# Moving the end waits for all DMAs from SyncE, ahead of the closing barrier, to GpSimd, between that barrier and the semaphore clearing

## The chip, the cores and the metric

The program runs on one core of a Trainium2 chip. The metric is the device time of one execution in microseconds. Executions of the same program mostly differ by up to about 1 us. The span of a profile is the time from the program's first instruction to its last. It is about 1.8 us shorter than the device time of the same run.

## The reference

The infinity norm of each row of an 8192 x 8192 float32 matrix, that is the largest absolute value of each row.

```python
def setup_inputs():
    rows = 8192
    cols = 8192
    return {"x": np.random.randn(rows, cols).astype(np.float32)}

def reference(x):
    return np.linalg.norm(x, ord=np.inf, axis=1)
```

So 268 MB are read once, and 32 KB are written.

## The kernel before

SyncE issues all loads, VectorE reduces each tile with a maximum of absolute values, and the last rows come in smaller and smaller pieces, so that little is left to reduce after the last load. Three stores write the result: `r_bulk` (rows of the large tiles) and `r_tail` from ScalarE's queue, and at the very end `r_fin`, one number per partition, 512 bytes, from SyncE's queue.

```python
    for i in range(0, n_tail, B):
        ...
                if last and k == k_last - 1:
                    absmax(r_tail[:, : n_tail - 1], part[:])
                    nc.scalar.dma_start(
                        out=out_t[:, : n_tail - 1], in_=r_tail[:, : n_tail - 1]
                    )
                    absmax(r_fin[:], t[:, at : B * cols + k_last - 1])
        ...
    nc.sync.dma_start(out=out_t[:, n_tail - 1 :], in_=r_fin[:])
    nc.at_finalize(start_first_load_early)
```

The end of the program is not written in the kernel; the framework adds it. In the built program of before it is, engine by engine. (A drain is the profile's DRAIN: VectorE's starts at 624.28 us, during the last reduction, and ends at 625.00 us, just after it. An event wait is an EVENT_SEMAPHORE instruction that waits for semaphores. A wait is met when its semaphore has the value that it waits for. In the list, 99 is VectorE's semaphore, 100 to 107 are those of the DMAs, 102 is the one that the last store raises, 96 and 97 belong to the barrier.)

```
SyncE : event wait (104, 103) ; event wait (105, 102) ; event wait (106, 101) ;
        event wait (107, 100) ; drain (99)              <- one drain with nine waits, split
all   : first barrier   (each engine: drain, raises 96; GpSimd: gather 96, release 97)
GpSimd: drain ; clear the range of semaphores
all   : second barrier
```

The drain with nine waits stands split in the built program: the drain keeps the first of its list (99), and the other eight go in pairs into event waits ahead of it. The nine waits keep the clearing behind the last update of every DMA's semaphore (the last store raises its own 16 times, and the last of these is called its completion below).

## Time and profile before

| | before |
|---|---|
| device time, median of six runs | 629.20 us (629.04 to 629.80) |
| span of the profiled run | 627.3 us |
| HBM read, rate over the span | 268.44 MB, 428 GB/s |
| VectorE busy | 552.7 us, 88% |
| issue of the last store to its landing | 1.4 us |

The page of the profile. Under it are the busy share of the DMA engines in 40 slices (tenths of a slice) and the rate in each.

```profile
span 627.3 us, 196 instructions
...
DVE 552.7 (88%) x58; POOL 0.2 (0%) x4
...
DMA  9999999999999999999999999999999999999996
GB/s 401 468 401 464 405 460 410 455 414 451 418 451 418 451 418 447 422 447 422 447 422 447 422 447 422 447 422 443 426 420 428 425 433 435 426 429 427 427 425 274
...
HBM read 268.44 MB, written 0.03 MB: 428 GB/s over the span
```

The DMA engines are busy in every slice but the last, at 401 to 468 GB/s, so the kernel is taken to be bound by the reads until its last few microseconds. The profile's chain of what ended last puts 64.1% on loads and 23.5% on the reductions into `r_bulk`, which free the buffers that later loads wait for; the change touches neither. The timeline of those (start, duration, engine, line, operation):

```profile
624.26 0.69 DVE L81 TENSOR_REDUCE r_fin<-t 128x1 f32<-128x517 f32 x1
624.98 0.35 SPq L117 DMA_DIRECT2D out_dram<-r_fin  x1
```

The last reduction ends at 624.96 us, SyncE issues the store at 624.98. The span still has 2.36 us to go. The view of waits for SyncE in the window from 624 us on (who waited for whom: us in total, times, longest):

```profile
SPq L117 <- DVE r_fin L81: 12.1, 1, 12.1
SPq L144 <- DMA out_dram<-r_fin: 1.0, 1, 1.0
SPq L144 <- PEq L144: 0.6, 2, 0.4
```

SyncE waits 1.0 us for the store (the second row); the third row is the two barriers. The instructions of the closing line, SyncE's from 625.43 to 626.45 us and then all of GpSimd's after 626 us (count, shortest/median/longest ns, first and last start):

```profile
L144 SPq EVENT_SEMAPHORE  x1: 968/968/968, 625.5 to 625.5; - x1
```

```profile
L144 POOLq EVENT_SEMAPHORE  x4: 17/17/17, 626.7 to 627.2; - x4
L144 POOLq DRAIN  x2: 34/52/70, 626.8 to 627.1; - x2
L144 POOLq EVENT_SEMAPHORE_RANGE_CLEAR  x1: 92/92/92, 626.9 to 626.9; - x1
```

SyncE's event wait of 968 ns holds the store's semaphore. Only after it come GpSimd's gather, which starts at 626.68 us, and its clearing, at 626.94 us.

### The profile page before, as it was taken

Reading aid. Unit: us, or ns where it says so; the run is one execution under the profiler, and the core shown is the slowest. Engines: PE = TensorE matmul, PEld = TensorE weight load, DVE = VectorE, ACT = ScalarE, POOL = GpSimd, SP = SyncE. Lnnn points to the kernel's source line nnn. Section 1 sums busy time; section 2 is a strip of 40 time slices with the busy share of each in tenths; the row PEclk is TensorE's granted clock in tenths of the full one; section 3 lists DMA queues with packets and bytes.
Section 4 is the critical chain, followed back from the end, with each engine's and each line's share of the span. In section 5 each row is a group of like instructions: output and inputs, shape, how many; then the busy total and the mean of one; then the engine's idle time right before and its main releaser. Section 6 shows DMA issues by size and latency. Waiting matters only on the chain.

```text
span 627.3 us, 196 instructions
## 1 busy us (share of the span) xinstructions
DVE 552.7 (88%) x58; POOL 0.2 (0%) x4
## 2 busy tenths in 40 slices
DVE  0588988889988889888898888998889999999998
POOL 0000000000000000000000000000000000000000
DMA  9999999999999999999999999999999999999996
GB/s 401 468 401 464 405 460 410 455 414 451 418 451 418 451 418 447 422 447 422 447 422 447 422 447 422 447 422 443 426 420 428 425 433 435 426 429 427 427 425 274
DMA packets 9138, 268.49 MB, mean 428 GB/s; under 512 B 1968, under 2 KB 1968, under 8 KB 2352
## 3 DMA queue, kind: packets, MB, share of 16 engines
q1 hardware_dynamic: 8208, 268.44, 99.2%
q10 hardware_dynamic: 928, 0.03, 0.1%
q14 instruction: 2, 0.02, 0.0%
HBM read 268.44 MB, written 0.03 MB: 428 GB/s over the span
## 4 chain that ended last, share of the span: by engine, by line
DMA 64%; DVE 30%; another core or an unknown queue 4%; issue 1%; SPq 0%
DMA t<-in_x_dram 64%; DVE r_bulk L81 24%; DVE part L81 5%; DVE t L81 1%; SPq L100 0%; DVE r_fin L81 0%
## 5 line engine op out<-in xcount | busy, mean ns | idle before, releaser
L81 DVE TENSOR_REDUCE r_bulk<-t 128x2 f32<-128x16384 f32 x24 | 413.3, 17220 | 69.7 <-DMA t<-in_x_dram 69.7
L81 DVE TENSOR_REDUCE part<-t 128x1 f32<-128x4096 f32 (+2 forms) x26 | 130.0, 5067 | 1.3 <-DMA t<-in_x_dram 1.3
L81 DVE TENSOR_REDUCE t<-t 128x1 f32<-128x2048 f32 (+2 forms) x5 | 8.6, 1746 | 0.3 <-DMA t<-in_x_dram 0.3
L78 DVE MEMSET part<- 128x60 f32 x1 | 0.1, 108 | 0.9 <-PEq L133 0.9
L81 DVE TENSOR_REDUCE r_fin<-t 128x1 f32<-128x517 f32 x1 | 0.7, 691 | 0.0
L81 DVE TENSOR_REDUCE r_tail<-part 128x15 f32<-128x60 f32 x1 | 0.2, 216 | 0.0
L133 POOL MEMSET const-bfloat16-1.0<- 128x1 bf16 x1 | 0.1, 101 | 0.0
L133 POOL MEMSET const-uint8-127<- 128x1 uint8 x1 | 0.1, 101 | 0.0
L133 POOL MEMSET const-float32-0.0<- 128x1 f32 x1 | 0.1, 98 | 0.2 <-issue 0.2
L133 POOL MEMSET const-float32-1.0<- 128x1 f32 x1 | 0.1, 98 | 0.0
## 6 DMA issues: line engine op xcount, KB each, us to landing
t<-in_x_dram SPq DMA_DIRECT2D x8, 4096.0 KB, 37.0
t<-in_x_dram SPq DMA_DIRECT2D x10, 2048.0 KB, 30.4
t<-in_x_dram SPq DMA_DIRECT2D x11, 1024.0 KB, 24.6
t<-in_x_dram SPq DMA_DIRECT2D x1, 512.0 KB, 15.9
t<-in_x_dram SPq DMA_DIRECT2D x2, 256.0 KB, 13.2
t<-in_x_dram SPq DMA_DIRECT2D x24, 40.7
out_dram<-r_bulk ACTq DMA_DIRECT2D x1, 24.0 KB, 57.9
out_dram<-r_tail ACTq DMA_DIRECT2D x1, 7.5 KB, 5.6
```

Source lines behind the costliest of these rows:

```text
L78: nc.vector.memset(part[:], 0.0)
L81: nc.vector.reduce_max(out=o, in_=i, axis=X, apply_absolute_value=True)
L133: nc = _bacc.Bacc("TRN2", target_bir_lowering=False, num_devices=1)
```

## The change

The intent: run the first barrier while the last store is still under way, and let only the clearing wait for the DMAs, on the reading that only the clearing needs them. The nine waits are taken off SyncE and put on a drain of GpSimd that takes the place of the drain ahead of the clearing. They are sorted so that the store's semaphore (`lane`) is the last of the list. SyncE's drain goes, and the drain ahead of the clearing is replaced, so the program has one drain fewer.

```diff
+def wait_for_stores_on_pool(nc):
+    sp, pool = mybir.EngineType.SP, mybir.EngineType.Pool
+    body, end = nc.main_func.blocks[-2:]
+    last_store = [ ... SyncE's DMA copies ... ][-1]
+    lane = last_store.sync_info.on_update[0].id
+    insts = end.instructions
+    src = next(i for i in insts if i.engine == sp)
+    ...
+    clear = next(k for k, i in enumerate(insts) if type(i).__name__ == "InstISA")
+    dst = insts[clear - 1]
+    ...
+    waits = sorted(src.sync_info.on_wait, key=lambda s: s.id == lane)
+    assert waits[-1].id == lane
+    wait = mybir.InstDrain(
+        name=nc.get_next_instruction_name(),
+        engine=pool,
+        ins=[],
+        outs=[],
+        sync_info=mybir.SyncInfo(on_wait=waits, on_update=[]),
+    )
+    insts = insts[: clear - 1] + [wait] + insts[clear:]
+    end.instructions = [i for i in insts if i.name != src.name]
 ...
     nc.at_finalize(start_first_load_early)
+    nc.at_finalize(wait_for_stores_on_pool)
```

In the built program this gives:

```
SyncE : (nothing)
all   : first barrier
GpSimd: event wait (105, 104) ; event wait (106, 103) ; event wait (107, 101) ;
        event wait (102, 100) ; drain (99) ; clear
all   : second barrier
```

## The prediction

> **What bounds the kernel.** HBM reads. The page shows 268.44 MB at a mean of 428 GB/s over a 627.3 us span, DMA in the 9s in every slice but the last. VectorE is busy 552.7 us (88%) and waits for loads. The change touches only the last 2 us.
>
> **The end now** (instructions of the closing line, by engine, and semaphore events, profiled run). VectorE ends r_fin at 624.97. SyncE issues the 512-byte store at 624.98, to 625.33. Its packets are done at about 626.03, its 16 completions arrive from 626.23 to 626.40. SyncE's drain with nine waits stands as four event waits of two semaphores each and a drain. The store's semaphore is in the second, which sits 968 ns, to 626.42. Then follow two more event waits (626.46, 626.52), the drain (626.59), SyncE's barrier drain (626.65), GpSimd's gather and release (626.68, 626.76), GpSimd's drain (626.84, 70 ns), the clearing (626.94, 92 ns) and the second barrier; the last instruction ends at 627.32. So 0.54 us pass from the store's last completion to the clearing, and 0.38 us from there to the end.
>
> **What the change does.** It removes SyncE's nine waits from ahead of the first barrier and puts them on a GpSimd drain between release and clearing, in place of the drain there, the store's semaphore sorted last. By the split seen before (the drain keeps the list's first wait, VectorE's; the rest go in pairs ahead of it) I expect the store's wait in the fourth of four event waits on GpSimd, directly ahead of the drain. Loads, reductions and stores stay.
>
> - First barrier: SyncE arrives at about 625.4 instead of 626.65; VectorE has arrived at 625.01. GpSimd releases by about 625.55. Three satisfied event waits at GpSimd's spacing of about 80 ns (626.68 to 626.76) end by about 625.85, 0.5 us before the store lands: hidden.
> - New chain after the last completion (626.40): GpSimd wakes and goes on, 0.1 us (before: last gather arrival 626.654 to the next event 626.756); drain to clearing 0.1 us (626.837 to 626.936). Clearing at about 626.60 instead of 626.94.
> - The second barrier is unchanged, 0.38 us.
>
> Saved: 0.54 - 0.20 = 0.34 us, all on the critical path, an estimate from these durations. The store's flight of 1.4 us stays exposed. The Trainium skill ("DMA: Bandwidth & Descriptors", Anatomy of one DMA) puts most of a DMA's fixed cost in the write receipt before the semaphore fires; here 0.2 to 0.37 us pass from the last packet to the completions.
>
> **Time.** 629.22 - 0.34 = 628.9 us, range 628.2 to 629.8. The three runs of before span 0.76 us, twice the gain, so a few runs may not resolve it. Faster by over 2% (12.6 us): 0.005. Within 2%: 0.99. Slower by over 2%: 0.005.
>
> **What would show it.** SyncE's 968 ns event wait is gone; GpSimd has one of 0.5 to 0.6 us in its fourth event wait; from r_fin's end to the last instruction 2.0 us instead of 2.35. Loads and reductions are unchanged.
>
> **What would make it wrong.** GpSimd wakes much slower from a DMA's semaphore than SyncE; the waits are lowered in another order, so that several 80 ns events follow the landing (gain down to 0.1 us); the store completes later; or the drift of reads between runs, up to about 1 us, covers the gain.

## The result, and the profile after

| | before | after |
|---|---|---|
| device time, median (range) of six runs | 629.20 us (629.04 to 629.80) | 628.88 us (628.68 to 629.48) |
| ratio, 95% interval | | 0.9994 (0.9981 to 1.0007) |
| span of the profiled run | 627.3 us | 627.2 us |
| end of the last reduction to the last instruction | 2.362 us | 2.003 us |
| last completion of the store to the clearing | 0.539 us | 0.174 us |

A ratio is the mean time of one kernel's runs over that of the other's of the same rounds, so it is not quite the ratio of the medians.

The page after:

```profile
span 627.2 us, 194 instructions
...
DVE 552.7 (88%) x58; POOL 0.2 (0%) x4
...
DMA  9999999999999999999999999999999999999996
...
HBM read 268.44 MB, written 0.03 MB: 428 GB/s over the span
```

Loads and reductions are as before. The span is only 0.09 us shorter, because in this profile the last reduction ended 0.27 us later, which the timeline shows beside that of before:

```profile
624.53 0.69 DVE L113 TENSOR_REDUCE r_fin<-t 128x1 f32<-128x517 f32 x1
625.25 0.35 SPq L149 DMA_DIRECT2D out_dram<-r_fin  x1
```

So the spans of two single profiles can't be subtracted here; the tail, from the end of this reduction, can. The waits of SyncE in the window from 624 us on:

```profile
SPq L149 <- DVE r_fin L113: 12.1, 1, 12.1
SPq L177 <- PEq L177: 1.3, 2, 1.2
```

SyncE no longer waits for the store. What it has instead is a wait of 1.2 us in a barrier, put down to the engine whose arrival the profile places last. That is the second barrier, which GpSimd now holds up. The instructions of SyncE's closing line from 625.5 to 626.01 us, then GpSimd's event waits (the compiler gives those that it split off a line of its own file), then GpSimd's other closing instructions from 625.9 us on:

```profile
L177 SPq DRAIN  x1: 123/123/123, 625.7 to 625.7; - x1
L177 SPq EVENT_SEMAPHORE  x1: 17/17/17, 625.9 to 625.9; - x1
```

```profile
bacc.py:44 POOLq EVENT_SEMAPHORE  x4: 43/43/43, 626.0 to 626.7; - x4
```

```profile
L177 POOLq EVENT_SEMAPHORE  x3: 17/17/17, 625.9 to 627.1; - x3
L177 POOLq EVENT_SEMAPHORE_RANGE_CLEAR  x1: 92/92/92, 626.8 to 626.8; - x1
L177 POOLq DRAIN  x1: 34/34/34, 627.0 to 627.0; - x1
```

The barrier's release at 625.9 us comes before the store has landed, the four event waits span from 626.0 to 626.7 us, and the clearing follows at 626.8. In full, from the records and the semaphore events of the two traces, counted from the end of the last reduction (us):

```
                                          before    after
store is issued                           +0.027   +0.027
SyncE arrives at the first barrier        +1.697   +0.556
GpSimd releases the first barrier         +1.800   +0.659
GpSimd's third event wait ends                 -   +0.976
store's last completion arrives           +1.441   +1.447
clearing starts                           +1.980   +1.621
last instruction of the program ends      +2.362   +2.003
last update of semaphore 2                +4.265   +3.908
```

The last row is outside the program's span. The Trainium skill ("Runtime: NRT & Kernel Launch", Semaphores 0–2 are reserved) says that semaphore 2 is the runtime's sync barrier, and in the trace its updates are the last events of an execution. From the first instruction to this last update are 629.22 us before, where the run's device time was 629.1 us. The difference is 0.12 us (0.118 to 0.127) in all 13 profiled runs, so this row is a way to see in one trace what the measured time sees. From the last instruction to it are 1.903 us before and 1.905 us after: what the tail lost, the execution, counted from the end of the last reduction, lost too.

### The profile page after: what moved, and what is told of

Read it like the earlier page. It is cut to its first block, busy times and chain, and to the rows that moved or that the text cites. A ratio compares the mean times of both kernels' runs of the same rounds, so it can differ in the third digit from the quotient of the medians.

```text
span 627.2 us, 194 instructions
## 1 busy us (share of the span) xinstructions
DVE 552.7 (88%) x58; POOL 0.2 (0%) x4
## 4 chain that ended last, share of the span: by engine, by line
DMA 64%; DVE 30%; another core or an unknown queue 4%; issue 1%; SPq 0%
DMA t<-in_x_dram 64%; DVE r_bulk L113 24%; DVE part L113 5%; DVE t L113 1%; SPq L132 0%; DVE r_fin L113 0%
```

## The experiments

**The theory.** The gain is made of two things. The barrier now runs under the store's flight of 1.42 us and costs nothing (position); and fewer event waits stand between the store's completion and the clearing (order of the waits). **Rivals:** the order alone is the gain (A); the position or the engine alone, the order being without effect (B); GpSimd is quicker to wake, or one hop between engines less is the gain (C); and the difference in time is drift of the reads.

Each kernel of the experiments gave a correct result. The device time is resolved to about 0.13% (0.8 us) by five rounds. "To clearing" is the time from the store's last completion to the start of the clearing. From the clearing to the last instruction it was 0.38 us wherever the second barrier stands. These values come from one profiled execution of each kernel; where a kernel was profiled twice (the change; e4 and e11), they agree to 2 ns.

| kernel | where the waits stand | event waits, from the store's own to the last | to clearing, us | median time, us | ratio (95%) |
|---|---|---|---|---|---|
| before | SyncE, ahead of barrier | 3, and SyncE's drain | 0.539 | | 1 |
| e2_sync_last | SyncE, ahead, sorted | 1, and SyncE's drain | 0.430 | 629.80 | 0.9999 (0.9987 to 1.0012) |
| e5_pool_ahead | GpSimd, ahead, sorted | 1, and a drain | 0.455 | 629.15 | 1.0000 (0.9987 to 1.0012) |
| e3_pool_unsorted | GpSimd, behind | 3, and a drain | 0.311 | 629.51 | 0.9997 (0.9984 to 1.0010) |
| the change (e1_after) | GpSimd, behind, sorted | 1, and a drain | 0.175 | 629.24 | 0.9992 (0.9978 to 1.0006) |
| e4_pool_on_drain | GpSimd, behind, on the drain | the drain alone | 0.087 | 629.24 | 0.9991 (0.9979 to 1.0004) |
| e6_pool_plus8 | the change, 8 event waits in place of 4 | 1, and a drain | 0.174 | 628.82 | 0.9996 (0.9984 to 1.0009) |
| e7_pool_plus24 | the change, 16 in place of 4 | 1, and a drain | 0.766 | 629.53 | 1.0003 (0.9989 to 1.0016) |
| e9_sync_plus8 | before, 4 more on SyncE | 3, SyncE's drain and 4 more | 0.789 | 629.41 | 1.0006 (0.9993 to 1.0018) |
| e10_sync_plus160 | before, 80 more on SyncE | 3, SyncE's drain and 80 more | 5.380 | 634.42 | 1.0076 (1.0064 to 1.0088) |

The first group (e1 to e4) ran on one chip, beside a kernel before of 629.75 us median; e5 to e9 (without e8) on another (629.21 us); e10, e8 and e11 on a third (629.49 us). The runs of before on the third chip hold one of 631.57 us. It lowers the ratios there: without it the ratio of the plain means is 1.0079 for e10, 0.9992 for e8 and 0.9998 for e11.

**e1_after: the change once more** (no edit).

> The change itself, once more, in five rounds. Theory (barrier hidden under the store's flight, and the store's wait directly ahead of the clearing): from the store's last completion to the start of the clearing 0.17 us (0.54 before), from it to the last instruction 0.56 us (0.92 before), and the time 0.2 to 0.5 us under the kernel before of the same rounds (about 0.9994). Rival (the time's difference is only drift of the reads): the same 0.17 us in the trace, but no difference in time.

Measured: 0.175 us to the clearing, 0.556 us to the last instruction, as in the first profile to 1 ns. The mean time is 0.43 us under before (629.22 against 629.65 us). Both intervals, here and in the first comparison, hold 1, so time alone does not settle it.

**e2_sync_last: the order alone.** The edit against the change:

```diff
-        engine=pool,
+        engine=sp,
...
-    insts = insts[: clear - 1] + [wait] + insts[clear:]
-    end.instructions = [i for i in insts if i.name != src.name]
+    at = next(k for k, i in enumerate(insts) if i.name == src.name)
+    end.instructions = insts[:at] + [wait] + insts[at + 1 :]
```

> The nine waits stay on SyncE ahead of the first barrier; only the order changes, the store's wait in the last event wait. Theory (order and position both count): two event waits of 64 ns no longer follow the completion, so last completion to clearing 0.54 - 0.13 = 0.41 us, time about 0.13 us under before. Rival A (order is all of the gain): 0.17 to 0.20 us, time like the change. Rival B (position or engine is all): 0.54 us.

Measured: 0.430 us. The order is worth 0.109 us in SyncE's place, not all of the gain and not nothing: rivals A and B fall. That it is 0.02 us more than the 0.41 expected is explained under e3. The profile's line of the split event waits of this kernel:

```profile
bacc.py:44 SPq EVENT_SEMAPHORE  x4: 28/28/28, 625.5 to 626.5; - x4
```

**e3_pool_unsorted: the position (with the engine), in the order of before.**

```diff
-    waits = sorted(src.sync_info.on_wait, key=lambda s: s.id == lane)
-    assert waits[-1].id == lane
+    waits = list(src.sync_info.on_wait)
```

> The waits on GpSimd after the first barrier as in the change, but in the order of before, so that the store's wait is in the second of four event waits. Theory: two event waits of about 90 ns now follow the completion: completion to clearing 0.17 + 0.18 = 0.35 us, time about 0.19 us under before. Rival A (order is all): 0.54 us. Rival B (position or engine is all): 0.17 us.

Measured: 0.311 us, between the rivals, but 0.04 us less than expected. The event waits of this kernel, to be read beside that of e2:

```profile
bacc.py:44 POOLq EVENT_SEMAPHORE  x4: 42/43/622, 626.5 to 627.4; - x4
```

Here one event wait took 622 ns, while in e2 and in the change all took 28 or 43 ns although one of them waited as long. The difference goes with the place within the pair, in all kernels here, though no run changed that place alone. In (105, 102) the store's semaphore is the second: 105 is met long before, and the instruction starts, holds through the store's flight and ends 30 ns after the completion. In (102, 100) it is the first: the instruction starts 24 ns after the completion, and takes its 43 ns then, so it ends at 67 ns. The change therefore loses 37 ns again that the old order did not have. Two event waits 87 ns apart, less these 37 ns, are 0.137 us, and that is what the change gains over e3 (0.311 less 0.174). The same holds on SyncE: 22 ns after the completion in before, 45 ns in e2, which is the 0.02 us more found there.

**e4_pool_on_drain: the store's wait on the drain itself.**

```diff
-    waits = sorted(src.sync_info.on_wait, key=lambda s: s.id == lane)
-    assert waits[-1].id == lane
+    waits = sorted(src.sync_info.on_wait, key=lambda s: s.id != lane)
+    assert waits[0].id == lane
```

> As the change, but the store's wait is put first in the list, which leaves it on the drain itself; no event wait follows the completion. Theory: 0.024 us to wake and about 0.10 us from the drain's start to the clearing, so 0.12 us instead of 0.17 us; time 0.05 us under the change, which five rounds will not resolve. Rival (a drain that waits is slower to go on than an event wait): 0.17 us or more.

Measured: 0.087 us, less than the 0.12 us expected. Since the drain keeps the first wait of its list, the store belongs first in the list, not last.

**e5_pool_ahead: the engine alone.** GpSimd waits, ahead of the first barrier's gather.

```diff
-    insts = insts[: clear - 1] + [wait] + insts[clear:]
+    gather = next(
+        k
+        for k, i in enumerate(insts)
+        if i.engine == pool and type(i).__name__ == "InstDrain"
+    )
+    insts = insts[:gather] + [wait] + insts[gather + 1 :]
```

> The waits on GpSimd, sorted as in the change, but ahead of the first barrier's gather: the engine changes, the barrier stays behind the store. Theory (the hidden barrier matters): after the completion come the event wait's end and the drain (0.15 us), the gather (0.08), release (0.08) and the drain ahead of the clearing (0.10): about 0.42 us to the clearing, time about 0.12 us under before. Rival C (GpSimd wakes faster, or one hop between engines less, is the gain): 0.17 to 0.20 us.

Measured: 0.455 us, 0.035 us over the 0.42 us expected and 0.025 us more than with the same waits on SyncE (e2). GpSimd as such is no faster at this; rival C falls. Its store's event wait in the profile:

```profile
bacc.py:44 POOLq EVENT_SEMAPHORE  x1: 43/43/43, 626.4 to 626.4; - x1
```

What is gained between this kernel and the change, 0.281 us, is what no longer stands between the waits and the clearing. The gather starts at 626.561 us, the drain ahead of the clearing at 626.720 and the clearing at 626.820. So 0.159 us of these are the gather and release of the barrier, and 0.100 us are that drain, which this kernel still has and whose place the waiting drain takes in the change. No run hid the barrier and kept both drains, so how much of the 0.100 us comes from the drain saved stays open.

**e6_pool_plus8 and e7_pool_plus24: how much fits under the store's flight.** Both put more waits that are met already on GpSimd, ahead of the store's; the compiler merged them in pairs, and eight of them share an event wait with a DMA's semaphore each (the store's is (102, 99) in both).

```diff
+    dve = next(s for s in waits if s.id == waits[0].id)
+    extra = [
+        mybir.InstEventSemaphore( ..., engine=pool, ...,
+            sync_info=mybir.SyncInfo(on_wait=[dve], on_update=[]))
+        for _ in range(8)     # 24 in e7
+    ]
-    insts = insts[: clear - 1] + [wait] + insts[clear:]
+    insts = insts[: clear - 1] + extra + [wait] + insts[clear:]
```

> The change with eight more waits that are met already, on GpSimd after the barrier and ahead of the store's wait; they are merged in pairs, so eight event waits in place of four. Theory (what precedes the store's wait is free as long as it ends before the store lands, 0.47 us of slack for 4 x 0.089 = 0.36 us): completion to clearing unchanged at 0.17 us, time like the change. Rival (every event wait on GpSimd costs its 89 ns): 0.53 us, time like before.

Measured: 0.174 us. Twice the event waits cost nothing.

> The same with 24 more waits, 16 event waits in place of four: 12 x 0.089 = 1.07 us against 0.47 us of slack. Theory: the store lands while GpSimd still works through them; completion to clearing 0.17 + 0.60 = 0.8 us, time 0.6 us over the change and about 0.25 us over before. Rival (event waits that are met cost nothing anywhere): 0.17 us.

Measured: 0.766 us. The last event wait now starts 0.616 us after the completion (627.763 less 627.147), so the store lands while GpSimd still works. The two lines of event waits, first of e6, then of e7 (the profile keeps eight of e7's sixteen; the other eight left no record, nor did the added ones of e9 and e10, so their number is that of the built program):

```profile
bacc.py:44 POOLq EVENT_SEMAPHORE  x8: 42/43/43, 625.7 to 626.4; - x8
```

```profile
bacc.py:44 POOLq EVENT_SEMAPHORE  x8: 43/43/43, 627.2 to 627.8; - x8
```

In e6 the seventh of eight event waits ended at 626.303 us, ahead of the completion (626.422 us); in e7 all eight that are seen start after it (627.147 us). The room under the flight is real and finite.

**e9_sync_plus8: the same in the place of before.** Eight more waits on SyncE, between its drain and the first barrier, in the kernel before. The edit is against the change, which it undoes.

```diff
-    insts = insts[: clear - 1] + [wait] + insts[clear:]
-    end.instructions = [i for i in insts if i.name != src.name]
+    dve = next(s for s in waits if s.id == 99)
+    at = next(k for k, i in enumerate(insts) if i.name == src.name)
+    extra = [
+        mybir.InstEventSemaphore( ..., engine=sp, ...,
+            sync_info=mybir.SyncInfo(on_wait=[dve], on_update=[]))
+        for _ in range(8)
+    ]
+    end.instructions = insts[: at + 1] + extra + insts[at + 1 :]
```

> The kernel before, with eight more waits that are met already (four event waits) on SyncE between its drain and the first barrier. Theory: each 64 ns stands behind the store's completion, so completion to clearing 0.54 + 0.26 = 0.80 us, time 0.26 us over before. Rival (such waits are free on SyncE as well): 0.54 us.

Measured: 0.789 us, so four event waits cost 0.250 us, where the change took four more for nothing (e6).

**e10_sync_plus160: does the time see the tail?** The same edit with `range(160)`.

> A calibration: the kernel before with 160 more waits that are met already (80 event waits in pairs) on SyncE between its drain and the first barrier. Theory (what stands behind the store's completion goes into the time one to one): 80 x 0.0625 us (the four of the small version took 0.25 us) = 5.0 us more from completion to clearing, so 5.54 us, and 5.0 us more time (ratio 1.008). Rival (the measured time does not see the tail, for instance because something outside the program's span ends later anyway): 5.5 us in the trace, less in the time.

Measured: 5.380 us to the clearing, 4.84 us more than before; the median time is 4.93 us more (634.42 against 629.49 us), the ratio 1.0076. The clearing of this kernel, beside 626.9 us in before:

```profile
L188 POOLq EVENT_SEMAPHORE_RANGE_CLEAR  x1: 92/92/92, 632.1 to 632.1; - x1
```

The tail goes into the time one to one within the noise. The rival that something else hides the tail falls.

**e8_one_barrier: the second barrier removed**, from the version e4.

```diff
-    insts = insts[: clear - 1] + [wait] + insts[clear:]
+    insts = insts[: clear - 1] + [wait] + insts[clear : clear + 1]
```

> The version with the store's wait on the drain itself, and the barrier after the clearing removed, so that GpSimd ends with the clearing and the other engines with the first barrier. It relies on the barrier that follows the program (updates of semaphore 2 in the trace, before other semaphores are reset), so it is an experiment and not a proposal. Theory: completion to clearing 0.087 us as measured there, then 0.092 us of clearing and the end: completion to the last instruction 0.18 us instead of 0.47 us, time 0.29 us under that version and about 0.74 us under before (ratio 0.9988). Rival (the second barrier is covered by what follows the program): the span is 0.29 us shorter, the time is not.

Measured: 0.088 us to the clearing and 0.180 us to the last instruction, against 0.471 us with the barrier (e11). The time was 629.05 us, 0.9988 of before (0.9976 to 1.0000), and 0.9992 without the run of 631.57 us, so it is not resolved. The lines of GpSimd's end, first of this kernel, then of e11, from 626 us on:

```profile
L177 POOLq EVENT_SEMAPHORE  x2: 17/17/17, 626.1 to 626.2; - x2
L177 POOLq EVENT_SEMAPHORE_RANGE_CLEAR  x1: 92/92/92, 627.1 to 627.1; - x1
```

```profile
L177 POOLq EVENT_SEMAPHORE  x4: 17/17/17, 626.4 to 627.6; - x4
L177 POOLq EVENT_SEMAPHORE_RANGE_CLEAR  x1: 92/92/92, 627.3 to 627.3; - x1
L177 POOLq DRAIN  x1: 34/34/34, 627.5 to 627.5; - x1
```

The clearing is now the last thing that the program does. Theory and rival each hold a part: of 0.291 us less in the span, the last update of semaphore 2 comes 0.196 us earlier (2.177 against 2.373 us after the completion). From the last instruction to it were 1.90 us in every other kernel, and 2.00 us here, so about 0.09 us were given back in what follows the program. It is no proposal: it leaves the order of the ends to what follows the program.

**e11_on_drain_again: the kernel e4 once more**, beside e8.

> The store's wait on GpSimd's drain itself, once more, beside the version without the second barrier on the same chip, and as the version that should beat both kernels: completion to clearing 0.087 us again, completion to the end 0.47 us against 0.56 us of the change and 0.92 us of before; time about 0.45 us under before (ratio 0.9993).

Measured: 0.088 us and 0.471 us, as before; the median time 629.36 us, ratio 0.9994 (0.9982 to 1.0006). In the trace this version beats both kernels, by 0.45 us and by 0.09 us; in time, neither lead is resolved.

## Why the prediction was right

The tail from the last reduction was predicted at 2.0 us and came at 2.003, for the reasons given. The time was predicted at 628.9 us and came at 628.88; that close a hit is luck, since the six runs span 0.8 us and the interval of the ratio is wider than the gain. Point by point:

- *Reads bound the kernel and the change touches only the last 2 us*: the second part is right, loads and reductions are unchanged; the first was not tested.
- *The barrier and the met waits are hidden under the store's flight, with 0.5 us to spare*: right. The third event wait ends 0.471 us before the completion, and e6 and e7 show that this room is what counts. One term was too small: SyncE was to arrive at the barrier 0.44 us after the reduction's end (625.4 us) and came at 0.556. Its barrier drain took 123 ns, directly behind the issue of a DMA; behind other waits, as in before, it took 7 ns. The 0.11 us were hidden too.
- *Last completion to the clearing 0.54 less 0.34, so 0.20 us*: it was 0.174. Its two terms were 0.1 us for GpSimd to wake and go on and 0.1 us from the drain to the clearing; the store's event wait starts 0.024 us after the completion, and 0.150 us later the clearing does. With no event wait in between (e4) the whole is 0.087 us. The parts of the gain, by experiments: order of the waits, on SyncE, 0.539 to 0.430 (0.109 us gained); the engine, 0.430 to 0.455 (0.025 us lost); the place behind the barrier with one drain fewer, 0.455 to 0.174 (0.281 us gained). Together 0.365 us. These steps depend on the order in which they are taken: with the old order the place and the engine together were worth 0.228 us (0.539 to 0.311).
- *The store's flight stays exposed*: right, 1.41 us before and 1.42 us after from issue to last completion.
- *GpSimd shows one event wait of 0.5 to 0.6 us*: wrong in form. The wait exists, as 0.495 us between the end of the third event wait (626.203) and the start of the fourth (626.698), but no record has that length, because the store's semaphore is the first of its pair. The old order on GpSimd did show one, of 622 ns. The Trainium skill ("Perfetto Trace Analysis", Sequencer-only Instruction) says that a record begins once all semaphores are met and that the wait is not in it. Taking an event wait for such an instruction, the trace agrees for the first wait of a pair (start 24 ns after the completion); for the second it does not (968 ns, 622 ns).
- *Few runs may not resolve it*: right. Both comparisons hold 1 in their interval. In the profiles of these kernels the last reduction ended anywhere from 624.92 to 625.87 us, a drift of the reads more than twice the gain. That the gain of 0.36 us reaches the measured time is concluded: the last update of semaphore 2 follows the tail to a few ns, every profiled run's device time ends up 0.12 us short of it, and e10 shows the same with a large tail. The times alone only agree with it.

## What to carry to other kernels

At the end of a kernel, ask what the last store's completion must really hold up, and put everything else (barriers, waits that are met already) under its flight; here that, with the new order and one drain fewer, was worth 0.36 us, and should be about as much in a short kernel that ends the same way (not tried). After the completion count instructions: the wait belongs on the very instruction that must follow, as its own wait, with none split off behind it (0.09 us more here). Where the change is smaller than the drift of the runs, measure from the last event ahead of it in the trace, and calibrate once with a version of it that is large enough to see.

## What the Trainium skill lacked or had wrong

- "Perfetto Trace Analysis" (Sequencer-only Instruction): the page has the record begin once all semaphores are met, but an event wait with two starts in the record while only the first is met, and the wait for the second is part of its duration: 968 ns on SyncE and 622 ns on GpSimd with the store's semaphore second, 28 and 43 ns with it first. The delay goes with this place too: the instruction ended 22 to 30 ns after the completion with the store's semaphore second, 45 to 68 ns with it first.
- No page that was read here has the spacing of met event waits with two semaphores each: 64 to 69 ns on SyncE between recorded ones (before, e2, e9), 60 to 63 ns as a mean over the unrecorded ones of e10 and e9, and mostly 87 ns on GpSimd. Nor the cost of a barrier drain directly behind a DMA issue: 123 ns against 7 ns on SyncE.
- "DMA: Bandwidth & Descriptors" (Anatomy of one DMA — SWDGE (gpsimd) path) puts about 2.0 us on the fixed part of a DMA, most of it the write receipt, from a fit for GpSimd's software path; the section has no such split for a store from SyncE's queue. Here that store, of 512 bytes, took 1.41 us: 0.84 us to the first packet, 0.20 us of packets, and 0.37 us from the end of the last packet to the last completion. So what can hold the receipt is less than half of this store; for GpSimd's path no run here shows it.
- "Runtime: NRT & Kernel Launch" (The ~15µs preamble/postamble breakdown) lists about 5 us after the kernel (1.5, 1.5 and 2). The trace shows 1.90 us from the program's last instruction to the last update of semaphore 2, and the time from the first instruction to this update is 0.12 us over the device time in all 13 profiled runs; what may follow, no run here shows. It does not say that dropping a program's own last barrier is partly given back there: 0.09 of 0.29 us.
